# Weight sums of every second feature: made in the output projection instead of the first up stage

## The chip, the cores and the metric

The kernel runs on one core of one Trainium2 chip. The metric is device time in microseconds (us) of one execution. Before the change the median of three runs is 2763.57 us (2761.47 to 2770.18). Engines: PE multiplies matrices (PEld loads its weights), DVE is the vector engine, ACT the scalar engine, POOL the GpSimd engine, SP the engine that here only issues transfers. Each engine works through its own queue in order; ACT, POOL and SP also issue DMA transfers from that queue.

## What is computed

One layer of a hybrid encoder on 2048 prompt rows and 8 x 16 sample rows: band attention and an mLSTM side by side, an output projection, then a convolutional feed-forward block.

```python
mix = jnp.concatenate([att, mlstm_out], axis=-1) @ w_out
x = x + rms_norm(mix, norm_g[1])
ffn, new_buf = conv_ffn(rms_norm(x, norm_g[2]), conv_buf, w_up, w_conv, b_conv, w_down)
x = x + rms_norm(ffn, norm_g[3])

def conv_ffn(h, buf, w_up, w_conv, b_conv, w_down):
    u = h @ w_up
    ext = jnp.concatenate([buf, u], axis=1)
    y = b_conv + sum(ext[:, j:j + S] * w_conv[j] for j in range(3))
    gate, up = jnp.split(y, 2, axis=-1)
    return (jax.nn.gelu(gate, approximate=True) * up) @ w_down, ext[:, S:]
```

w_up is 1024 x 5632, that is 22 features of 128 for each of gate and up; w_down is 2816 x 1024. All data are float32.

## The kernel before, in words

**Products.** Every matrix product is made as three matmuls on a high and a low part (`mm3`, lines 104 to 106): an ACT cast makes the high part, a DVE subtraction the low part (`split`, lines 1308 and 1309). The up product of a feature does not multiply four quarter blocks eight times but seven times, by sums of blocks. For each feature f the four blocks of w_up (quads a11, a12, a22, a21, each 128 x 512, 256 KB) need four sums s1 to s4.

**Stages.** After the projections and while the attention still ends, `project` (w_out) runs over 17 row tiles. Each tile has two halves of 512 columns with 8 x 3 matmuls each; `mt` holds the transposed rows of a tile (PE transposes `mT_pt`, ACT cast at line 210, DVE low part at line 211), `mx` takes a half's sum from PSUM (line 1026), `mr` is the scaled input of a later tile. Beside the tiles of the second half, units of `h2_units` prepare the feed-forward input (`x2r`, `h2T_pt`, `B`). Then come three row blocks, each with an up stage over 22 features and a down stage. Block 0's down stage takes two halves (dh) of 22 k-steps with 18 matmuls each; blocks 1 and 2 use a seven-product form of the down product too, which needs folded blocks of w_down, kept in `wtd`.

**Where sums are made.** In block 0, `load_quads` loads a feature's four quads through SP (line 1320), makes s1 to s4 on DVE (line 1325) and stores them through POOL to `wsd` (line 1327); blocks 1 and 2 load quads and stored sums back (line 1336). The generator `folds` does the like for the 11 blocks of w_down, during block 0's down stage, one step after each k-step: at step 0 two loads on ACT's queue (line 1175), at step 1 the other two, at step 3 four operations on DVE (line 1180) and four stores on POOL (line 1185). Its tiles come from the pool `spare` with six places, used in turn; `quad` has 11 places.

**What sets the order.** The kernel is written as generators that are interleaved by hand; a scheduler then orders each engine's queue. Instructions wrapped in `keep_in_program_order` keep their place in the order in which the program was written.

Of the kernel before, what the change touches and what calls it, by code (L numbers as in the profile page):

```python
# [39 lines left out]
PAIRS = [[(((b[j], 0), (b[j + 3], 0)), j * P, P, f"{b[j]}") for j in range(3)] for b in FBLOCKS[:2]]  # L40
NK = NF // 2
FAST = (1, 2)
ORDERS = [[f for k in range(NK) for f in (k, k + NK)] if b in FAST else list(range(NF)) for b in range(3)]
# [6 lines left out]
def hymba_step(ctx: ExitStack, tc: tile.TileContext, I: dict, O: dict):  # L50
# [923 lines left out]
    def project(tiles):  # L974
# [25 lines left out]
        def turn_rows(s):  # L1000
            rows_to_T(s.m, s.mt, 0, f"mT{s.t}", ps_mm if s.t < 8 else ps_big)

        load(ss[0])
        norm(ss[0])
# [4 lines left out]
        for n_, s in enumerate(ss):  # L1009
# [7 lines left out]
            for hf in range(2):  # L1017
                c = slice(hf * 512, hf * 512 + 512)
                acc = ps_mm(f"wo{t}_{hf}")
                for k in range(KT):  # L1020
                    mm3(acc, s.mt[:, 0, k, :], s.mt[:, 1, k, :], wo[k][0][:, c], wo[k][1][:, c],
                        start=(k == 0), stop=(k == KT - 1))
                    if k % 4 == 3:
                        yield 2.6, 0.5
                ssq = small.tile([P, 1], F32, tag="wssq", name=f"wssq{t}_{hf}")
# [12 lines left out]
            nc.vector.scalar_tensor_tensor(xr, m, rs, xr, op0=ALU.mult, op1=ALU.add)  # L1038
            nc.sync.dma_start(x2d[t], xr)


# [124 lines left out]

    def folds(period, plan):

        live = {}

        def load(k, xs):
            if k < NK:
                for x in xs:
                    live[k, x] = spare_tile(f"fold{k}_{x}")
                    tc.keep_in_program_order(nc.scalar.dma_start(live[k, x], I["w_down"][k][:, x * 512:(x + 1) * 512]))

        def combine(k):
            a, b, c, d = [live[k, x] for x in range(4)]
            for o, x, y in ((a, b, a), (b, c, b), (c, a, c), (d, d, c)):
                tc.keep_in_program_order(nc.vector.tensor_tensor(o, x, y, op=ALU.add if o is d else ALU.subtract))  # L1180

        def store(k):
            if k >= 0:
                for x in range(4):
                    tc.keep_in_program_order(nc.gpsimd.dma_start(wtd[k][:, x * 512:(x + 1) * 512], live.pop((k, x))))
# [127 lines left out]
    def load_quads(b, f, g):  # L1313

        src = lambda i: I["w_up"][f][:, i * 512:(i + 1) * 512]
        if b == 0 and g == 0:
            q = []
# [11 lines left out]
            return [a11, s2, s3, s1]  # L1329
        if b == 0:  # L1330
            return raws.pop(f)
# [125 lines left out]
    unfinished = []  # L1457
    fold = folds(4, {0: ("ab",), 1: ("cd",), 3: ("combine", "store")})

# [6 lines left out]
    for b, tiles in enumerate(FBLOCKS):  # L1466
# [344 lines left out]
        for dh in range(2):  # L1811
# [9 lines left out]
            for c in range(6):  # L1821
# [35 lines left out]
                for k in ks:  # L1857
                    if (dh, k) not in parts:
                        split_g(dh, k, w3_tile)
                    if dh == 1 or k >= 3:  # L1860
                        fetch(dh + (k + 2) // NF, (k + 2) % NF)
                    for j in order if k == NF - 1 else range(nt):
                        down(j, k, wh, wl)
                    if k >= 1:
                        ahead.step()
                    if b == 0:
                        next(fold, None)
            if tail:
                continue
# [117 lines left out]
```

## Time and profile before

| | |
|---|---|
| median of three runs | 2763.57 us |
| the profiled execution's own time | 2763.96 us |
| its span, first to last instruction | 2762.2 us, mean granted clock 0.997 |
| PE busy in the span | 2692.4 us (97%) |
| DVE, ACT, POOL busy | 1902.5 us (69%), 1437.1 us (52%), 627.4 us (23%) |
| DMA traffic | 539.72 MB, mean 195 GB/s |
| w_out, its matmuls | from 1053.9 to 1318.3 us |
| block 0, up stage | from 1319.4 to about 1640 us |
| block 0, down stage | from 1639.2 to about 1839 us |

The profile is one execution. A row of a stretch of time gives, for each engine, its busy time and the count of its instructions in that stretch. A row of waits reads: who waited, for whom, us in total, how often, the longest. A row of a tile gives the shortest, middle and longest duration in ns and the first and last start in us. A row of the timeline gives start, duration, engine, line and operation, and in brackets how long the engine had idled and what ended that. A transfer's time to landing runs from its issue until its data are there.

### The profile page before, as it was taken

To read this page: it belongs to the slowest core of one execution; us is meant where nothing else is said; L and a number is where in the kernel's file an instruction comes from. 1 tells how busy PE (TensorE), PEld (TensorE's weight loads), DVE (VectorE), ACT (ScalarE), POOL (GpSimd) and SP (SyncE) were. 2 spreads that over 40 slices of the span, in tenths; PEclk is the share of its full clock that TensorE was granted. 3 is DMA by queue.
4 is the path that set the end of the run, shared out by engine and by line. 5 is a ranking of instruction groups with operands and counts; after the bars stand their busy time and mean duration, and the time that the engine had idled before them with its cause. 6 is when DMAs were issued, how large, how long until landed. Compare 5 with 4: busy or idle time off the path is not lost.

```text
span 2762.2 us, 47713 instructions
## 1 busy us (share of the span) xinstructions
PE 2692.4 (97%) x16422; PEld 2520.0 (91%) x16422; DVE 1902.5 (69%) x3593; ACT 1437.1 (52%) x2918; POOL 627.4 (23%) x1276
## 2 busy tenths in 40 slices
PE   7899999999999999999999999999999999999998
PEld 7899999998899998888999998789999878999976
DVE  5345445646546567655999988558888875998956
ACT  4355545635356566544554555435554665555554
POOL 1000010211100011222333322123443212555401
PEclk9999999999999999999999999999999999999999
DMA  5534355547564456355645559867886777788775
GB/s 180 161 117 137 106 158 166 170 146 215 155 187 132 139 169 196 120 171 177 239 166 182 166 174 337 297 230 202 242 241 189 244 238 245 217 261 247 249 264 184
DMA packets 329185, 539.72 MB, mean 195 GB/s; under 512 B 60354, under 2 KB 162974, under 8 KB 328814
## 3 DMA queue, kind: packets, MB, share of 16 engines
q1 hardware_dynamic: 248382, 393.82, 46.1%
q0 software_dynamic: 35632, 97.48, 11.3%
q10 hardware_dynamic: 44928, 45.37, 5.0%
q8 instruction: 129, 2.11, 0.3%
q14 instruction: 114, 0.93, 0.1%
HBM read 383.28 MB, written 162.68 MB: 198 GB/s over the span
## 4 chain that ended last, share of the span: by engine, by line
PE 79%; DMA 10%; DVE 5%; ACT 2%; issue 2%; POOL 1%; SPq 0%; ACTq 0%; DVEq 0%; POOLq 0%
PE uec L104 6%; PE uec L105 6%; PE uec L106 6%; PE dn L106 4%; PE dn L104 4%; PE dn L105 4%; PE ua L106 3%; PE ua L105 3%; PE ua L104 3%; PE qb L105 2%; PE qb L106 2%; PE qb L104 2%; PE pt L76 2%; PE wo L106 2%; PE wo L105 2%
## 5 line engine op out<-in xcount | busy, mean ns | idle before, releaser
L104 PE MATMUL uec<-B,wuh 128*128 128x384 f32 (+1 forms) x720 | 236.0, 328 | 2.5 <-DVE uu L1645 2.5
L105 PE MATMUL uec<-B,wuh 128*128 128x384 f32 (+1 forms) x720 | 235.1, 327 | 0.0
L106 PE MATMUL uec<-B,wul 128*128 128x384 f32 (+1 forms) x720 | 233.7, 327 | 0.0
L1308 ACT CAST wuh<-wu 128x512 fp32r<-128x512 f32 x255 | 141.7, 618 | 107.8 <-PE uec L105 98.6
L1309 DVE TENSOR_TENSOR wul<-wu,wuh 128x512 fp32r<-128x512 f32 x255 | 165.1, 683 | 3.7 <-DMA x2d<-mx 2.3
L405 DVE CUSTOM_DVE_ANT_0 tmp<-s,nb 128x640 f32<-128x640 f32 (+4 forms) x128 | 94.4, 737 | 93.9 <-PE s L395 92.1
L104 PE MATMUL vo<-wi_h,hT 128*128 128x256 f32 x544 | 155.2, 285 | 0.7 <-DVE mt L211 0.6
L106 PE MATMUL vo<-wi_h,hT 128*128 128x256 f32 x544 | 155.6, 286 | 0.0
L105 PE MATMUL vo<-wi_l,hT 128*128 128x256 f32 x544 | 154.8, 285 | 0.0
L104 PEld LDWEIGHTS uec<-B,wuh 128*128 128x128 f32 x720 | 135.1, 188 | 5.4 <-DVE uu L1645 4.1
L104 PE MATMUL qk<-hT,wi_h 128*128 128x384 f32 (+1 forms) x384 | 128.5, 335 | 7.4 <-ACT qk_st L236 6.7
L105 PEld LDWEIGHTS uec<-B,wuh 128*128 128x128 f32 x720 | 135.2, 188 | 0.2
L106 PEld LDWEIGHTS uec<-B,wul 128*128 128x128 f32 x720 | 135.1, 188 | 0.0
L418 DVE TENSOR_TENSOR ptl<-pt,pth 128x640 fp32r<-128x640 f32 (+4 forms) x128 | 93.6, 738 | 57.4 <-ACT pth L417 56.4
L406 ACT ACTIVATE tmp<-tmp,mn 128x640 f32<-128x640 f32 (+4 forms) x128 | 97.6, 763 | 66.1 <-DVE mn L405 64.7
L1309 DVE TENSOR_TENSOR wdl<-wdr,wdh 128x512 fp32r<-128x512 f32 x198 | 125.0, 685 | 7.8 <-ACT wdh L1308 7.6
L105 PE MATMUL qb<-hT,wi_h 128*128 128x384 f32 (+1 forms) x384 | 127.9, 333 | 0.0
L105 PE MATMUL qk<-hT,wi_h 128*128 128x384 f32 (+1 forms) x384 | 127.8, 333 | 0.0
L106 PE MATMUL qk<-hT,wi_l 128*128 128x384 f32 (+1 forms) x384 | 127.4, 332 | 0.0
L106 PE MATMUL qb<-hT,wi_l 128*128 128x384 f32 (+1 forms) x384 | 127.3, 331 | 0.0
L104 PE MATMUL qb<-hT,wi_h 128*128 128x384 f32 (+1 forms) x384 | 127.2, 331 | 0.0
L106 PE MATMUL dn<-wdh,al 128*128 128x512 f32 x308 | 124.1, 403 | 2.6 <-DVE al L1309 2.6
(447 smaller groups left out, 9271.1 us busy)
## 6 DMA issues: line engine op xcount, KB each, us to landing
wu<-in_w_up SPq DMA_DIRECT2D x220, 256.0 KB, 4.9
wu<-wsd SPq DMA_DIRECT2D x176, 256.0 KB, 5.0
wdr<-in_w_down SPq DMA_DIRECT2D x110, 256.0 KB, 5.3
wi_raw<-in_w_in SPq DMA_DIRECT2D x52, 512.0 KB, 4.0
wsd<-ws POOLq DMA_DIRECT2D x88, 256.0 KB, 3.8
wdr<-wtd SPq DMA_DIRECT2D x88, 256.0 KB, 5.3
gr<-gd SPq DMA_DIRECT2D x39, 384.0 KB, 6.1
kraw<-kTd SPq DMA_DIRECT2D x112, 128.0 KB, 3.3
```

Source lines behind the costliest of these rows:

```text
L76: nc.tensor.transpose(out, in_, ident[:n, :n])
L104: nc.tensor.matmul(out, ah, bh, start=start, stop=False, skip_group_check=onto)
L105: nc.tensor.matmul(out, ah, bl, start=False, stop=False, skip_group_check=onto)
L106: nc.tensor.matmul(out, al, bh, start=False, stop=stop, skip_group_check=onto)
L405: nc.vector.tensor_tensor_reduce(o_, s_, b_, 1.0, 3e38, ALU.add, ALU.min, accum_out=mn)
L406: nc.scalar.activation(tmp[:, :n], tmp[:, :n], AF.Exp, bias=mn, scale=-1.0, accum_out=rsum[:, i % 4, hh:hh + 1])
L418: nc.vector.tensor_tensor(s.ptl[:, sl, qc], ptv, s.pth[:, sl, qc], op=ALU.subtract)
L1308: nc.scalar.copy(h, r)
L1309: nc.vector.tensor_tensor(l, r, h, op=ALU.subtract)
```

## The change

`folds` becomes a generator over a list of units and now makes both kinds of sums: "T" for a block of w_down, "U" for a feature of w_up. It advances by six steps for a unit: two loads, nothing, two loads, and then one DVE operation a step; the fourth operation and the four stores come at the first step of the next unit. `project` advances a "U" fold for the odd features (`UPS`) by one step after each four k's of a half, which makes four steps to a tile and 68 in all, against 66 for the 11 units. In block 0, `load_quads` then treats an odd feature as blocks 1 and 2 do: it loads quads and stored sums, seven loads in place of four, and makes no sums. In block 0's down stage the "T" fold is advanced once after each even k-step and twice after each odd one, so that a unit still takes four k-steps.

```diff
+UPS = [1, 3, 5, 7, 9, 11, 13, 15, 17, 19, 21]
+WOUT_FOLDS = [("U", f) for f in UPS]
...
+        fold, owed = folds(WOUT_FOLDS), [0.0]
         load(ss[0])
...
                     if k % 4 == 3:
+                        owed[0] += 6 * len(WOUT_FOLDS) / 66
+                        while owed[0] >= 1:
+                            owed[0] -= 1
+                            next(fold, None)
                         yield 2.6, 0.5
...
+        for _ in fold:
+            pass
...
-    def folds(period, plan):
...
-        acts = dict(ab=lambda k: load(k, (0, 1)), cd=lambda k: load(k, (2, 3)), combine=combine, store=store,
-                    before=lambda k: store(k - 1))
-        for k in range(NK):
-            for step in range(period):
-                for what in plan.get(step, ()):
-                    acts[what](k)
+    def folds(units):
+
+        keep = tc.keep_in_program_order
+        sub, plus = ALU.subtract, ALU.add
+        ahead = None
+        for n_, (what, k) in enumerate(units):
+            src, dst = (I["w_down"], wtd) if what == "T" else (I["w_up"], wsd)
+            part = lambda d, x: d[k][:, x * 512:(x + 1) * 512]
+            if ahead:
+                ahead()
+            q = [spare_tile(f"fold{what}{k}_{x}") for x in range(2)]
+            for x in range(2):
+                keep(nc.scalar.dma_start(q[x], part(src, x)))
+            yield
+            yield
+            q += [spare_tile(f"fold{what}{k}_{x}") for x in (2, 3)]
+            for x in (2, 3):
+                keep(nc.scalar.dma_start(q[x], part(src, x)))
+            yield
+            a, b, c, d = q
+            if what == "T":
+                ops = [(a, b, a, sub), (b, c, b, sub), (c, a, c, sub), (d, d, c, plus)]
+                out = [a, b, c, d]
+            else:
+                ops = [(c, d, c, plus), (d, a, d, sub), (a, c, a, sub), (b, b, a, sub)]
+                out = [a, d, c, b]
+            for o, x, y, op in ops[:3]:
+                keep(nc.vector.tensor_tensor(o, x, y, op=op))
                 yield
-        if live:
-            store(NK - 1)
+
+            def ahead(out=out, dst=dst, k=k, last=ops[3]):
+                o, x, y, op = last
+                keep(nc.vector.tensor_tensor(o, x, y, op=op))
+                for i, t in enumerate(out):
+                    keep(nc.gpsimd.dma_start(dst[k][:, i * 512:(i + 1) * 512], t))
+        ahead()
...
-        if b == 0 and g == 0:
+        if b == 0 and g == 0 and f not in UPS:
...
-        if b == 0:
+        if b == 0 and f not in UPS:
             return raws.pop(f)
...
-    fold = folds(4, {0: ("ab",), 1: ("cd",), 3: ("combine", "store")})
+    fold = folds([("T", k) for k in range(NK)])
...
                     if b == 0:
                         next(fold, None)
+                        if k % 2:
+                            next(fold, None)
```

The line numbers of the changed kernel are higher: by 2 in the first thousand lines, by 7 in the tail of `project`, by 9 in `h2_units`, by 16 from `load_quads` on. What stands on three engines at one place of w_out, near the change of stages to the feed-forward block, is shown next.

DVE in w_out, around the sample tile (16) while `mt8`, the next tile's rows, is made; `mx16` takes tile 16's two halves from PSUM, `x2r` are rows of `h2_units`. Before:

```order
L997 TENSOR_SCALAR mr8_15162<-mr8_15162,att8_rs_15203 128x512
L1026 TENSOR_TENSOR mx16_15206<-wo16_0_15208,norm_row1_13117 128x512
L1098 SCALAR_TENSOR_TENSOR x2r0_15263<-x2r0_15263,n2_0_rs_15286,g2_15160 128x1024
L1098 SCALAR_TENSOR_TENSOR x2r3_15265<-x2r3_15265,n2_3_rs_15292,g2_15160 128x1024
L211 TENSOR_TENSOR mt8_15198<-mT8_pt0_15237,mt8_15198 128x1024
L1026 TENSOR_TENSOR mx16_15206<-wo16_1_15250,norm_row1_13117 128x512
```

And with the change:

```order
L999 TENSOR_SCALAR mr8_15237<-mr8_15237,att8_rs_15287 128x512
L1203 TENSOR_TENSOR foldU11_2_15305<-foldU11_3_15306,foldU11_2_15305 128x512
L1033 TENSOR_TENSOR mx16_15290<-wo16_0_15292,norm_row1_13117 128x512
L1107 SCALAR_TENSOR_TENSOR x2r0_15353<-x2r0_15353,n2_0_rs_15377,g2_15235 128x1024
L1107 SCALAR_TENSOR_TENSOR x2r3_15355<-x2r3_15355,n2_3_rs_15383,g2_15235 128x1024
L213 TENSOR_TENSOR mt8_15282<-mT8_pt0_15326,mt8_15282 128x1024
L1203 TENSOR_TENSOR foldU11_3_15306<-foldU11_0_15257,foldU11_3_15306 128x512
L1033 TENSOR_TENSOR mx16_15290<-wo16_1_15339,norm_row1_13117 128x512
```

The first sum of feature 11, which needs the third and the fourth quad, stands ahead of tile 16's first evacuation and of `mt8`; the second sum stands ahead of the second evacuation.

ACT one tile later, in tile 8; `wssq` are the squares of a half, `b2` and `B` belong to `h2_units`. Before:

```order
L1123 COPY b220_15394<-h2T_pt0_1_1_15389 128x512
L1028 ACTIVATE mx8_15311,wssq8_0_15349<-wo8_0_15313 128x512
L1118 CAST B1_0_15280<-t20_15396 128x4x128
L1118 CAST B2_0_15281<-t30_15397 128x4x128
L210 CAST mt9_15303<-mT9_pt0_15353 128x1024
```

And with the change:

```order
L1035 ACTIVATE mt16_15149,wssq16_1_15385<-wo16_1_15339 128x512
L997 ACTIVATE mt9_15394,assq9_15395<-mr9_15337 128x512
L1188 DMA foldU13_0_15422<-in_w_up 128x512
L1188 DMA foldU13_1_15423<-in_w_up 128x512
L1127 CAST B1_0_15371<-t20_15500 128x4x128
L1127 CAST B2_0_15372<-t30_15501 128x4x128
L1193 DMA foldU13_2_15489<-in_w_up 128x512
L1193 DMA foldU13_3_15490<-in_w_up 128x512
L1035 ACTIVATE mx8_15402,wssq8_0_15449<-wo8_0_15404 128x512
L212 CAST mt9_15394<-mT9_pt0_15453 128x1024
```

The four loads of feature 13 stand in ACT's queue ahead of the squares of tile 8's first half and of the cast of `mt9`.

PE at the same place, in the second half of tile 8 (`wo8_1`), with the transposes for tile 9 (`mT9_pt0`). Before:

```order
L105 MATMUL wo8_1_15376<-wo3_13516,mt8_15198 128x512
L106 MATMUL wo8_1_15376<-wo3_13516,mt8_15198 128x512
L76 MATMUL mT9_pt0_15353<-ident_72,mr9_15248 128x128 x8
L104 MATMUL wo8_1_15376<-wo3_13516,mt8_15198 128x512
L105 MATMUL wo8_1_15376<-wo3_13516,mt8_15198 128x512
```

And with the change:

```order
L106 MATMUL wo8_1_15476<-wo6_13592,mt8_15282 128x512
L107 MATMUL wo8_1_15476<-wo6_13592,mt8_15282 128x512
L78 MATMUL mT9_pt0_15453<-ident_72,mr9_15337 128x128 x8
L108 MATMUL wo8_1_15476<-wo6_13592,mt8_15282 128x512
L1115 MATMUL h2T_pt0_0_1_15522<-ident_72,x2r0_15353 128x128 x4
L106 MATMUL wo9_0_15552<-wo0_13379,mt9_15394 128x512
L107 MATMUL wo9_0_15552<-wo0_13379,mt9_15394 128x512
```

Before, twelve matmuls of `wo8_1` and a group of four transposes stand between `mT9_pt0` and the first use of `mt9`; with the change one matmul and that group.

More of the change, by code (lines that the diff above doesn't have):

```diff
@@ L1165, in late_B @@
             nc.vector.tensor_tensor(lo, lo.bitcast(F32), hi, op=ALU.subtract)
-    def folds(period, plan):
[L1169 to L1185, printed above, removed]
-        acts = dict(ab=lambda k: load(k, (0, 1)), cd=lambda k: load(k, (2, 3)), combine=combine, store=store,
-                    before=lambda k: store(k - 1))
-        for k in range(NK):
-            for step in range(period):
-                for what in plan.get(step, ()):
-                    acts[what](k)
-                yield
-        if live:
-            store(NK - 1)
```

## The prediction

> **What bounds the kernel now.** I read the stages first: busy time by engine in the three stretches that the change touches (w_out with the tail of the attention, the up stage of block 0, the down stage of block 0). Columns: span, then PE, PEld, DVE, ACT, POOL busy with counts, clock, DMA share, GB/s.
>
> ```profile
> 1053.00:1312.00 259.00, 255.51 (x1389) 215.40 (x1389) 159.32 (x296) 129.90 (x313) 62.60 (x119) 1.00 0.50 161
> 1312.00:1645.00 333.00, 331.96 (x1878) 326.85 (x1877) 306.17 (x465) 169.90 (x273) 111.99 (x193) 1.00 0.54 183
> 1645.00:1865.00 220.00, 214.61 (x992) 179.16 (x991) 149.35 (x217) 104.50 (x182) 48.94 (x95) 1.00 0.84 285
> ```
>
> PE sets the end in all three, at full granted clock. It idles 259.00 - 255.51 = 3.5 us in w_out, 1.0 us in up 0 and 5.4 us in down 0: together 9.9 us, and no rearrangement of DVE, ACT or DMA work can win more than that here. DVE, at 306 of 333 us, is nearly full in up 0, yet PE hardly waits for it; its room is in w_out (99.7 us idle). Then I read what PE waited for, w_out first, then down 0 (us in total, times, longest).
>
> ```profile
> PE wo L106 <- DVE mt L211: 1.2, 3, 0.5
> PEld wo L106 <- DVE mt L211: 2.4, 3, 0.9
> ...
> PE dn L104 <- DVE fr L1393: 2.0, 2, 1.5
> PE h2T_pt L1106 <- ACT b L1123: 1.7, 1, 1.7
> PE h2T_pt L1106 <- DVE t L1132: 0.8, 1, 0.8
> ```
>
> In w_out the wait that recurs is for mt, the transposed rows of the next tile. So I followed one late tile (start, duration, engine, line): transposes, ACT cast, DVE low part, and the evacuation that shows when the second half of the current tile has ended on PE.
>
> ```profile
> 1252.23 1.04 PE L76 MATMUL mT_pt<-ident,mr 128*128 128x128 f32 x8
> ...
> 1253.36 1.02 ACT L210 CAST mt<-mT_pt 128x1024 fp32r<-128x1024 f32 x1 [2.59 <-PE mT_pt L76]
> ...
> 1254.41 1.23 DVE L211 TENSOR_TENSOR mt<-mT_pt,mt 128x1024 fp32r<-128x1024 f32 x1 [4.41 <-ACT mt L210]
> ...
> 1256.75 0.68 DVE L1026 TENSOR_TENSOR mx<-wo,norm_row 128x512 f32<-128x512 f32 x1
> ```
>
> The low part is done at 1255.64, and wo's second half at about 1256.75: a margin of 1.1 us before PE stands. That is thin, although DVE had idled 4.41 us just before. The rows of six such tiles give the pace and the cover:
>
> ```profile
> L210 ACT CAST mt<-mT_pt x6: 1006/1014/1016, 1227.6 to 1292.7; 128x1024 fp32r<-128x1024 f32 x6
> ...
>   ACT mt L210: 19.1, 6
> ```
>
> (1292.7 - 1227.6) / 5 = 13.0 us a tile; DVE idles 19.1 / 6 = 3.2 us a tile just before mt. With four fold steps to a tile, a step is 3.25 us.
>
> **The change, part by part.** First, what leaves up 0. The sums of one feature are four DVE operations and four POOL issues:
>
> ```profile
> L1325 DVE TENSOR_TENSOR ws<-wu,wu x44: 678/683/693, 1304.4 to 1611.3; 128x512 f32<-128x512 f32 x44
> 1312.00:1645.00 333.00, 56.66 (x84) 1.00 0.54 183
> L1327 POOL DMA_DIRECT2D wsd<-ws x84 | 45.7, 544 | 86.0 <-DVE ws L1325 82.4 <-DVE ug L1483 2.1 <-DVE x L1622 0.7
> ```
>
> Half of the 22 features go, 44 operations x 0.683 = 30.1 us of DVE (84 of the 88 lie inside the stretch, the rest just before it) and 44 x 0.544 = 23.9 us of POOL. SP gets three loads more for each odd feature, 33 in all; SP issues them ahead, and the stage's DMA share of 0.54 has room, since 44 stores leave it. What the path can gain is PE's idle time in the stage, at least 0 and at most 1.0 us. I take -1.0. Where cover is concerned: an odd feature's stored sums must have landed before SP's in-order queue reaches them; they were stored tens of us earlier, except feature 21's, which is used last.
>
> Second, what enters w_out: 44 ACT loads, 44 DVE operations, 44 POOL stores. In volume it fits: 159.3 + 30.1 = 189 of 259 us of DVE. The price is in order, since these are in-order queues with waits. A unit takes six steps: first two loads (and the last sum and four stores of the unit before) at step 0, the other two loads at step 2, three sums at steps 3, 4, 5. The pool of spare tiles has six places, so the loads at step 2 reuse the places of quads whose stores were issued at step 0, and ACT stands until those have landed; the sum at step 3 needs exactly these loads, and DVE stands until they have. The nearest rows for the parts of this chain:
>
> ```profile
> L1175 ACTq DMA_DIRECT2D fold<-in_w_down x44: 334/335/852, 1649.8 to 1825.2; - x44
> L1180 DVE TENSOR_TENSOR fold<-fold,fold x44: 674/684/694, 1656.8 to 1838.5; 128x512 f32<-128x512 f32 x44
> L1185 POOL DMA_DIRECT2D wtd<-fold x44: 542/542/608, 1661.3 to 1839.5; - x44
> ...
> DMA to landing us min/median/max: 3.1/6.4/9.7
> ```
>
> Those are the folds of the down stage; the weight sums' own stores and the weight loads (median us from issue to landing; the first store row is of up 0, the second of w_out's end):
>
> ```profile
> wsd<-ws POOLq DMA_DIRECT2D x84, 256.0 KB, 3.7
> wsd<-ws POOLq DMA_DIRECT2D x4, 256.0 KB, 6.5
> wu<-in_w_up SPq DMA_DIRECT2D x220, 256.0 KB, 4.9
> ```
>
> Last sum 0.68, four store issues 4 x 0.54 = 2.17 (the fourth store is that of the quad whose place is wanted last), landing 3.7 to 6.5, load issue 0.33, landing 4.9: 11.8 to 14.6 us after step 0, while step 3 comes 3 x 3.25 = 9.8 us after it. So DVE stands 2.0 to 4.8 us at the first sum of a late unit, and behind it in its queue are mx (the evacuation of wo) and mt, for which PE waits. The cover is DVE's own idle time ahead of mt, 3.2 us, plus the margin of 1.1: 4.3 us. The excess is 0 at the one end and 0.5 us at the other; without that cover (the hold falls on top of the tile's other work) it is 4.8 - 1.1 = 3.7 us. Bounds over 11 units: 0 to 41 us. A gain is excluded, as nothing leaves this stage. I take 0.6 us a unit, next to the covered end because the idle before mt is in every one of the six rows, and a little above it because a sum of 0.68 itself also falls between two steps of the chain: 11 x 0.6 = 6.6 us. The place on PE where the transposes now stand one wo matmul and four short transposes ahead of their use is inside this: cast 1.02 and low part 1.23 against a margin that has gone.
>
> A rule of the Trainium skill speaks on this chain. DMA: Bandwidth & Descriptors, section "Anatomy of one DMA", fits a transfer as 2.0 us plus its bytes over 436 GB/s; my estimate from that page is 2.6 us for 256 KB, and the chain would be 0.68 + 2.17 + 2.6 + 0.33 + 2.6 = 8.4 us, inside the 9.8, so that nothing would wait. The trace differs: its medians are 3.7 to 6.5. The sum by that rule would be -1.0 instead of +5.6.
>
> Third, down 0. Bursts of four sums become single sums; loads, stores and volume stay. But the distance from the stores of a unit to the loads that reuse their places shrinks from two k-steps to one. A k-step is the distance of two gh casts, and ACT already waits here for such stores (us, times, longest):
>
> ```profile
> 1732.99 0.83 ACT L1308 CAST gh<-gr 128x768 fp32r<-128x768 f32 x1 [3.33 <-PE dn L105]
> 1737.14 0.84 ACT L1308 CAST gh<-gr 128x768 fp32r<-128x768 f32 x1 [1.24 <-PE dn L105]
> ACT gh L1308 <- DMA wtd<-fold: 13.6, 3, 4.9
> ```
>
> So each of 11 units has 4.15 us less. Behind the standing loads are gh and wdh, the next weights' casts. The lower bound is -5.4 (all PE idle gone, the single sums leave room at the boundary of the two halves, where 1.5 + 1.7 + 0.8 of it lies). For the upper, today's 13.6 us of such waits stand beside at most 5.4 us of PE idle, a ratio of 0.4; 11 x 4.15 x 0.4 = 18 us. I take 0: the instructions of ACT and DVE stand almost as before, casts run two k-steps ahead, and the boundary wait comes from SP's loads, which do not move.
>
> Sum: -1.0 + 6.6 + 0 = +5.6 us on the profiled execution's 2763.96 us (span 2762.2), so 2769.6; that execution lies 0.4 above the median of the runs, 2763.57, which gives **2769 us**.
>
> **The rivals.**
>
> 1. All covered. Stores and loads land as fast as the shortest of the weight sums' transfers in this trace,
>
> ```profile
> DMA to landing us min/median/max: 2.3/3.8/9.7
> ```
>
> so the chain is 0.68 + 2.17 + 2.3 + 0.33 + 2.3 = 7.8 us, under 9.8, nothing waits in w_out, and up 0 gives its 1.0: 2763. For it: DVE's 99.7 us of idle time in w_out. Against it: the medians. Chance 0.18. The Trainium skill's fit, named above, leads here too.
> 2. The boundary in down 0 goes as well, 4.0 us, and most of the rest of PE's 9.9: 2754 to 2757. Against it: SP's order there. Beyond -0.3% it needs 8.3 of 9.9 us. Chance 0.08.
> 3. Slower: DVE is held at the first sum, with mt behind it. The place is DVE in w_out's late tiles; it decides from a store landing of about 6 us on, as with w_out's own four stores (6.5), when the cover of 4.3 us is used up. Priced midway between the covered excess and the uncovered one, (0.5 + 3.7) / 2 = 2.1 us a unit, it is 11 x 2.1 = 23 us, less 1.0 of up 0: 2786. For it: the margin of only 1.1 us. Against it: DVE's idle time before mt. Chance 0.28.
> 4. Slower in down 0: ACT stands at the reused places, and PE's dn follows. Half of the bound, 9 us, on top of the forecast's 5.6: 2778. For it: the 13.6 us of today. Against it: the loads' place in ACT's order, which stays. Chance 0.12.
>
> That the change does not do what it says is no rival: the diff removes the sums of the odd features from up 0 and makes the same four in w_out.
>
> **How the numbers follow.** The forecast, a loss between 0 and 8 us, has the remaining 0.34; its own range is 2763 to 2772. A measurement of this kernel can tell about 0.3%, or 8.3 us, from no change. Faster by more than that is rival 2, 0.08; within it lie the forecast and rival 1, 0.34 + 0.18 = 0.52; slower are rivals 3 and 4, 0.28 + 0.12 = 0.40. The range for 8 in 10 runs from 2757, where rival 2 ends, to 2790, a little above rival 3.
>
> **What would show it.** In up 0: DVE busy about 276 of some 333 us, PE idle under 1 us, sums down to x44. In w_out: 44 sums of 0.68, DVE busy near 189, waits of DVE for the fold's loads and of ACT for the stores, PE waits for mt up from 1.2 to some 6 us; if there are none, rival 1 holds, and if they pass 20 us, rival 3. In down 0: the wait of gh for wtd's stores near 13.6; doubled, with dn behind, it is rival 4. The prediction is wrong if up 0 shortens by more than 2 us (PE then had hidden cost there) or if the span changes outside 1053 to 1865.

## The result: slower, and the profile after

The changed kernel takes 2800.44 us (median of 6 runs, 2796.05 to 2805.34), the kernel before 2767.06 us beside it (6 runs). The ratio is 1.0125, with a 95% interval of 1.0113 to 1.0137: 33 us slower. The profiled execution of the changed kernel took 2805.32 us, its span is 2803.6 us.

The stages come first, each from its own first matmul to that of the next: w_out, up stage of block 0, down stage of block 0. The rows of the down stage end 2.2 us ahead of that, in both kernels alike. The columns are span, then PE, PEld, DVE, ACT and POOL busy with counts, clock, DMA share, GB/s. Before:

```profile
1053.90:1319.40 265.50, 262.01 (x1416) 220.50 (x1415) 162.06 (x301) 129.87 (x314) 62.80 (x120) 1.00 0.51 165
1319.40:1639.20 319.80, 319.10 (x1823) 316.75 (x1822) 297.00 (x450) 166.73 (x267) 110.83 (x190) 1.00 0.54 181
1639.20:1836.90 197.70, 191.97 (x857) 155.77 (x856) 136.72 (x196) 93.09 (x157) 38.26 (x73) 1.00 0.86 289
```

The same stages of the changed kernel:

```profile
1052.30:1352.50 300.20, 273.75 (x1415) 227.58 (x1414) 184.54 (x342) 129.06 (x314) 84.83 (x165) 0.96 0.67 219
1352.50:1671.40 318.90, 317.93 (x1824) 317.29 (x1823) 278.37 (x414) 168.02 (x267) 73.57 (x146) 1.00 0.54 176
1671.40:1876.10 204.70, 195.57 (x857) 158.70 (x856) 135.37 (x194) 93.18 (x157) 35.68 (x70) 0.97 0.83 279
```

w_out is 34.7 us longer, up 0 is 0.9 shorter, down 0 is 7.0 longer; what lies ahead of w_out is 1.6 shorter and what lies behind down 0 is 2.2 longer. Together that is 41.4 us, the difference of the two spans (2803.6 - 2762.2); the profiled execution stands 4.9 us above its median, that of the kernel before 3.1 below its own.

The 34.7 us of w_out have two halves that are read differently. PE's idle time went from 265.50 - 262.01 = 3.5 to 300.20 - 273.75 = 26.5 us, 23.0 more. And PE's busy time grew by 11.7 us with the same matmuls (1416 counted before, 1415 after): the granted clock of the stage is 0.96 where it was 1.00. What PE waited for in w_out (us in total, times, longest):

```profile
PE wo L108 <- DVE mt L213: 7.8, 2, 4.1
PE h2T_pt L1115 <- DVE x2r L1107: 7.4, 1, 7.4
PE ot L432 <- ACT pth L419: 3.9, 1, 3.9
```

So it is not a little at each unit: four stops (3.9, 7.4, 4.1 and 3.8) make 19 of the 26.5 us. They lie at three places.

**Tile 1, near 1085 us.** ACT's timeline before:

```profile
1080.68 0.37 ACT L715 ACTIVATE num<-ma,colsp 128x129 f32<-128x129 f32 x1 [3.74 <-DVE cst L713]
1081.52 1.29 ACT L417 CAST pth<-pt 128x640 fp32r<-128x640 f32 x2 [0.47 <-PE ot L430]
...
1083.70 0.41 ACT L660 ACTIVATE mvo<-mvo 128x256 f32<-128x256 f32 x1
```

and in the changed kernel:

```profile
1082.62 0.37 ACT L717 ACTIVATE num<-ma,colsp 128x129 f32<-128x129 f32 x1 [2.01 <-DVE cst L715]
1083.22 0.60 ACT L1035 ACTIVATE mx<-wo 128x512 f32<-128x512 f32 x1 [0.23 <-DVE mx L1033]
...
1086.28 0.42 ACT L662 ACTIVATE mvo<-mvo 128x256 f32<-128x256 f32 x1 [2.38 <-DMA mvo<-vobd]
...
1087.19 0.67 ACT L419 CAST pth<-pt 128x640 fp32r<-128x640 f32 x1
```

pth (the attention weights of the last heads, for which PE's `ot` waits) stood directly behind num. Now mx and mvo stand between, mvo waits 2.38 us for its load (vobd, which is no load of the folds), and pth comes 4.6 us behind num instead of 0.8. The scheduler has put ACT's instructions into another order around the fold's loads.

**Tile 8, 1218 to 1234 us.** DVE's timeline at the first sum of a unit; its last two loads were issued on ACT's queue from 1217.89 on:

```profile
1227.99 0.69 DVE L1203 TENSOR_TENSOR foldU<-foldU,foldU 128x512 f32<-128x512 f32 x1 [8.56 <-DMA foldU<-in_w_up]
1228.60 0.68 DVE L1033 TENSOR_TENSOR mx<-wo,norm_row 128x512 f32<-128x512 f32 x1
1232.04 1.28 DVE L1107 SCALAR_TENSOR_TENSOR x2r<-x2r,n_rs,g 128x1024 f32<-128x1024 f32 x1 [2.75 <-POOL n_rs L95]
```

DVE stands 8.56 us: ACT had waited 1.3 us before it issued the two loads (1216.6 to 1217.9), and some 9 us passed until the sum had them. Behind it is mx, behind mx is ACT's mx (12.78 us idle), then the square sums of x2r, POOL's n_rs, DVE's x2r, and PE at last. Over w_out DVE stood at sums for loads in six of the eleven units:

```profile
DVE foldU L1203 <- DMA foldU<-in_w_up: 19.4, 6, 8.6
```

What PE did after that stop (start, duration):

```profile
1233.47 1.09 PE L1115 MATMUL h2T_pt<-ident,x2r 128*128 128x128 f32 x4 [7.39 <-DVE x2r L1107]
1234.21 0.78 PE L106 MATMUL wo<-wo,mt 128*128 128x512 f32 x1
1234.78 0.63 PE L107 MATMUL wo<-wo,mt 128*128 128x512 f32 x1
...
1238.58 0.39 PE L106 MATMUL wo<-wo,mt 128*128 128x512 f32 x1
```

The same matmul takes 0.78, 0.63 and, five us later, 0.39 us: the clock is lower after the stop and comes back. The next unit's first sum held DVE 4.11 us at 1254, with mt right behind it: PE's stop of 4.1. Here the loads were issued late: ACT stood 5.77 us around them, by the trace until the stores from the places that they reuse had landed. ACT and DVE (the cast for mt ends at 1250.30):

```profile
1244.68 2.33 ACTq L1193 DMA_DIRECT2D foldU<-in_w_up  x2
1247.11 0.60 ACT L1035 ACTIVATE mx<-wo 128x512 f32<-128x512 f32 x1 [5.77 <-DMA wsd<-foldU]
1249.28 1.02 ACT L212 CAST mt<-mT_pt 128x1024 fp32r<-128x1024 f32 x1 [1.48 <-PE mT_pt L78]
1254.33 0.69 DVE L1203 TENSOR_TENSOR foldU<-foldU,foldU 128x512 f32<-128x512 f32 x1 [4.11 <-DMA foldU<-in_w_up]
1254.94 1.22 DVE L213 TENSOR_TENSOR mt<-mT_pt,mt 128x1024 fp32r<-128x1024 f32 x1
```

**The last tile, near 1336 us.** Here the held operation is not a fold but the up stage's own first sum, whose load landed late; it held DVE 2.90 us in the kernel before:

```profile
1336.02 0.69 DVE L1341 TENSOR_TENSOR ws<-wu,wu 128x512 f32<-128x512 f32 x1 [5.63 <-DMA wu<-in_w_up]
...
1338.55 1.22 DVE L213 TENSOR_TENSOR mt<-mT_pt,mt 128x1024 fp32r<-128x1024 f32 x1
```

The clock in slices of 10 us around two of the stops:

```profile
1220.00:1230.00 10.00, 6.08 (x31) 4.68 (x29) 1.29 (x2) 0.63 (x3) 0.00 (x0) 1.00 0.90 319
1230.00:1240.00 10.00, 6.47 (x25) 5.25 (x26) 7.25 (x10) 6.83 (x14) 3.67 (x7) 0.66 0.11 32
...
1250.00:1260.00 10.00, 5.26 (x13) 3.65 (x14) 5.89 (x8) 4.39 (x10) 3.04 (x8) 0.76 0.92 328
```

The DMA share of 0.90 with 319 GB/s in the first slice is the burst in which the loads of the first hold landed: x2r, g and x2d of the other work are in flight with them.

### The profile page after: what moved, and what is told of

It reads as the page before. It is cut to its first block, busy times and chain, and to the rows that moved or that the text cites. A ratio compares the mean times of both kernels' runs of the same rounds, so it can differ in the third digit from the quotient of the medians.

```text
span 2803.6 us, 47833 instructions
## 1 busy us (share of the span) xinstructions
PE 2706.6 (97%) x16422; PEld 2529.4 (90%) x16422; DVE 1904.9 (68%) x3593; ACT 1437.2 (51%) x2918; POOL 613.3 (22%) x1276
## 4 chain that ended last, share of the span: by engine, by line
PE 45%; DMA 5%; DVE 2%; issue 1%; ACT 1%; POOL 1%; SPq 0%; DVEq 0%; POOLq 0%; ACTq 0%
PE uec L106 5%; PE uec L107 5%; PE uec L108 5%; PE dn L108 3%; PE dn L106 3%; PE dn L107 3%; PE ua L108 3%; PE ua L107 3%; PE ua L106 3%; PE dnm L108 1%; PE ub L106 1%; PE ub L108 1%; PE ub L107 1%; PE dnm L107 1%; PE dnm L106 1%
## 5 line engine op out<-in xcount | busy, mean ns | idle before, releaser
L1324 ACT CAST wuh<-wu 128x512 fp32r<-128x512 f32 x284 | 156.7, 617 | 107.6 <-PE uec L107 98.2
L1325 DVE TENSOR_TENSOR wul<-wu,wuh 128x512 fp32r<-128x512 f32 x284 | 183.3, 686 | 2.3 <-ACT wuh L1324 1.2
L1325 DVE TENSOR_TENSOR al<-ar,ah 128x768 fp32r<-128x768 f32 (+2 forms) x94 | 71.0, 765 | 81.4 <-ACT ah L1324 81.1
```

The lines of the kernel that those rows point to most:

```text
L1324: nc.scalar.copy(h, r)
L1325: nc.vector.tensor_tensor(l, r, h, op=ALU.subtract)
```

## The experiments

The theory at first was: a sum reads loads that were issued one step earlier, DVE stands there, and the units cost 2 to 3 us each. Its rivals were the DVE volume, the traffic, the reused places and the down stage. In the diffs, "old folds" stands for the generator and the plan of the kernel before, kept for block 0's down stage.

| run | change against before | ratio, 95% interval | us | w_out of the profiled execution |
|---|---|---|---|---|
| changed kernel | all | 1.0125 (1.0113 to 1.0137) | +33.4 | 300.2 |
| u_only | new sums in w_out | 1.0110 (1.0092 to 1.0128) | +30.8 | 296.5 |
| t_only | new folds in down 0 | 1.0002 (0.9990 to 1.0013) | +0.2 | 264.5 |
| dve_only | 44 sums, no transfers | 1.0012 (1.0003 to 1.0022) | +3.4 | 268.6 |
| stores_only | 44 stores on POOL | 1.0025 (1.0011 to 1.0039) | +6.9 | 267.6 |
| loads_only | 44 loads on ACT | 1.0065 (1.0047 to 1.0083) | +18.2 | 278.7 |
| moves_only | loads and stores | 1.0075 (1.0058 to 1.0091) | +20.0 | 280.4 |
| loads_pool | 44 loads on POOL | 0.9998 (0.9988 to 1.0008) | -1.7 | 266.3 |
| loads_sp | 44 loads on SP | 1.0027 (1.0018 to 1.0036) | +8.1 | 270.6 |
| loads_tiny | 44 loads of 8 KB on ACT | 1.0003 (0.9994 to 1.0012) | +1.2 | 266.7 |
| loads_first | u_only, load three steps ahead | 1.0104 (1.0083 to 1.0125) | +30.3 | 282.3 |
| u_skip8 | u_only, three steps left out | 1.0117 (1.0095 to 1.0138) | +29.9 | 280.0 |
| u_skip8_again | the same kernel | 1.0099 (1.0079 to 1.0119) | +27.8 | 282.0 |
| early4 | four units, tiles 1 to 7 | 1.0029 (1.0017 to 1.0040) | +8.5 | 267.0 |
| u_late_start | u_only, started six steps later | 1.0029 (1.0018 to 1.0040) | +8.2 | 272.7 |
| u_pool | u_only, loads on POOL | 1.0034 (1.0017 to 1.0052) | +12.9 | 272.4 |
| u_sp | u_only, loads on SP | 1.0068 (1.0053 to 1.0083) | +19.9 | 281.0 |
| u_loads_free | u_only, loads placed by the scheduler | 1.0092 (1.0077 to 1.0107) | +25.6 | 283.8 |
| u_free | u_only, all placed by the scheduler | 1.0091 (1.0069 to 1.0114) | +25.5 | 265.2 |

"us" is the difference of the medians of the run and of the kernel before, run beside it; the ratio is worked out otherwise, and for u_pool it gives 9.4 us instead of 12.9. The last column is of one execution each and stands at 265.5 in the kernel before. It need not follow the medians. What lies ahead of w_out, where only u_loads_free and u_free place units, took 1046.5 to 1055.5 us in the other profiled executions, so a few us of a total need not be the effect of a version.

### Which part: u_only and t_only

```diff
 u_only, in block 0:
-    fold = folds([("T", k) for k in range(NK)])
+    fold = folds_old(4, {0: ("ab",), 1: ("cd",), 3: ("combine", "store")})
 t_only:
-UPS = [1, 3, 5, 7, 9, 11, 13, 15, 17, 19, 21]
+UPS = []
```

> The sums of the 11 odd features are made in w_out as in the change, but block 0's down stage keeps its old plan of folds (two k-steps from store to reload, four sums in one burst). If the loss belongs to w_out (PE's idle time there grew from 3.5 to 26.5 us and its busy time by 12 us at a lower granted clock), this run keeps nearly all of it: 26 to 36 us above the kernel before, PE idle in w_out over 15 us, and PE idle in down 0 back near 5.7 us. If the down stage carried it, at most 15 us above.

> No odd feature is moved (w_out and up 0 as before); only block 0's down stage makes its folds one operation at a time, with one k-step from store to reload. If the loss belongs to w_out: 0 to 6 us above the kernel before, with PE idle in down 0 near 9 us and DVE waiting there for the fold's loads (9.1 us in the changed kernel). If the shorter distance is a main cost: 12 us or more above.

Both as expected of the loss in w_out: 30.8 us in the one, 0.2 in the other. PE's idle time in w_out is 25.2 us in u_only, in three of the four stops of the changed kernel (7.4, 4.1, 4.3) and a smaller fourth (2.1). The folds one operation at a time cost nothing alone; PE's idle time in t_only's down 0 is 5.3 us, not the 9 expected. In the changed kernel down 0 took 7.0 us more, with one stop of 3.7 us; the two ratios differ by 0.0015, 4 us, inside their intervals, so whether that is in every execution is open.

### Volume: dve_only, stores_only, loads_only, moves_only

```diff
 the kernel before, in project, after each four k's:
+                        next(extra, None)
 dve_only, at steps 3, 4, 5 and 6 of a unit:
+                keep(nc.vector.tensor_tensor(t, t, t, op=ALU.subtract))
 loads_only and moves_only, two at steps 0 and 2:
+                keep(nc.scalar.dma_start(t, I["w_up"][f][:, x * 512:(x + 1) * 512]))
 stores_only and moves_only, four at the next unit's step 0:
+                keep(nc.gpsimd.dma_start(wsx[f - 2][:, x * 512:(x + 1) * 512], t))
```

> The kernel before, with 44 more DVE sums of one 128x512 tile in w_out at the steps where the change makes its sums; they read a tile that was filled once, so no load, no store and no wait for a transfer comes with them. Late loads as the cause: the 30 us of DVE work alone fit into DVE's 100 us of idle time, -2 to +6 us. DVE volume, or one more operation ahead of mt, as the cause: 15 us or more above.

> The kernel before with 44 stores on POOL's queue in w_out, four at every sixth step, from tiles filled once, to a scratch tensor; no loads, no sums. If the stores carry the cost of the moves (POOL's statistics stand behind 4 x 0.54 us of issues, and the traffic of the bursts of four): 10 us or more above the kernel before. If the loads carry it: -2 to +5 us. If only both together fill the queues, this run and the one with loads alone stay each under 6 us.

> The kernel before with the change's 44 loads on ACT's queue in w_out at the same steps, no sums and no stores. The moves with loads and stores cost 20.0 us. If the loads in ACT's queue (its order around them, and their traffic) carry that: 10 us or more above the kernel before, with PE standing for pth near 1085 us again (3.5 us). If the stores on POOL's queue carry it: -2 to +5 us.

> The kernel before, with the change's 44 loads on ACT's queue and 44 stores on POOL's queue in w_out at the same steps, to a scratch tensor, and no sums. If DVE standing at a sum whose load is late is the cause, PE loses little here: 0 to 12 us above the kernel before. If the traffic itself (transfers of x, of vobd and of the first weights that land later) or ACT standing at reused places is the cause: 20 us or more above.

DVE volume is excluded as the cause (+3.4). The theory misses in moves_only: 20.0 us without a single sum. The loads carry 18.2 of them, as the one side of their expectation had it; the stores' 6.9 lie between their two bounds, and the parts do not add up (18.2 and 6.9 alone, 20.0 together). In loads_only PE's stops in w_out were:

```profile
PE ot L430 <- ACT pth L417: 3.5, 1, 3.5
PE wo L106 <- DVE mt L211: 3.1, 2, 2.8
```

the first and the last place, without tile 8's. That left the bytes and the queue.

### Bytes or queue: loads_pool, loads_tiny, loads_sp

```diff
-                keep(nc.scalar.dma_start(t, ...))
+                keep(nc.gpsimd.dma_start(t, ...))      loads_pool
+                keep(nc.sync.dma_start(t, ...))        loads_sp
+                keep(nc.scalar.dma_start(t[:, 0:16], ...))   loads_tiny
```

> The kernel with loads alone, its 44 loads issued on POOL's queue instead of ACT's; same steps, same bytes, no sums, no stores. With loads on ACT's queue the scheduler placed pth, for which PE's next product waits, behind mx and mvo in ACT's order near 1085 us; in this kernel ACT's order there is that of the kernel before. If ACT's order around the loads carries the 18.2 us: +3 to +9 us (what 44 issues on POOL cost in the run of stores alone, 6.9), with no stop for pth. If the bytes of the loads, which make other transfers land later, carry it: +14 us or more.

> The kernel with loads alone on ACT's queue, each load cut to 16 of 512 columns (8 KB instead of 256 KB). If the bytes carry the 18.2 us: -2 to +5 us. If the issues in ACT's queue and the order that the scheduler makes around them carry it: +10 us or more, with stops at other places than 1220 and 1320 us.

> The kernel before with 44 loads of 256 KB on SP's queue in w_out, no sums, no stores. No instruction is added to ACT's queue, but the scheduler's order of ACT near 1085 us has mx and mvo ahead of pth, as with loads on ACT's queue; with loads on POOL's queue it had not, and cost 0. If that order by itself stops PE: PE stands for pth there (2 us or more), and the total is 6 us or more above the kernel before. If only loads in ACT's own queue do it: no stop for pth and under 4 us.

The bytes by themselves are excluded: loads_pool moves the same 44 x 256 KB at the same steps, the stage's DMA share is up from 0.51 to 0.66, and nothing is lost.

```profile
1054.30:1320.60 266.30, 262.47 (x1414) 220.09 (x1413) 161.28 (x301) 130.03 (x314) 87.69 (x165) 1.00 0.66 208
```

loads_sp shows the first place alone. It adds nothing to ACT's queue, but the scheduler puts mx (here ahead of num as well) and mvo ahead of pth there too, and PE stands:

```profile
1080.69 0.58 PE L430 MATMUL ot<-pth,vhl 128*128 128x256 f32 x1 [3.92 <-ACT pth L417]
```

It costs 8.1 us, and no other stop of w_out in it is longer than 0.8 us. Its w_out is 5.1 us longer than before; where the other 3 us lie is not shown. Nor does mvo ahead of pth stop PE every time. In loads_tiny, whose order is another again (mvo ahead of pth, mx behind), ACT stood longer for it, and PE's wait for pth was 0.6 us:

```profile
1082.43 0.42 ACT L660 ACTIVATE mvo<-mvo 128x256 f32<-128x256 f32 x1 [4.43 <-DMA mvo<-vobd]
```

loads_tiny costs nothing: the issues by themselves are free. By its own expectation that speaks for the bytes; together with loads_pool it says that neither the issues nor the bytes cost anything alone, and that full loads in ACT's or SP's queue do, with the orders made around them. Order and bytes changed together there, so it decides no more. loads_only's further 10 us over loads_sp are loads in ACT's own queue and the orders made around them; ACT stood once for 5.0 us at such a load. Which of the two it is stays open.

### The distance from load to sum: loads_first and u_skip8

```diff
 loads_first:
-            q = [spare_tile(f"fold{what}{k}_{x}") for x in range(2)]
-            for x in range(2):
+            q = [spare_tile(f"fold{what}{k}_{x}") for x in range(4)]
+            for x in range(4):
                 keep(nc.scalar.dma_start(q[x], part(src, x)))
 u_skip8:
-                        owed[0] += 6 * len(WOUT_FOLDS) / 66
+                        owed[0] += 0 if (n_, hf, k) in ((8, 0, 7), (8, 1, 3), (8, 1, 7)) else 1
```

> Sums of the 11 odd features in w_out, the down stage's folds by the old plan. A unit issues its four loads at step 0, makes two sums at step 3 and two at step 4 with the four stores; so each sum reads a load of at least three steps before (about 10 us in the late tiles) instead of one, while the distance from a store to the load that reuses its place stays two steps. If DVE standing at a sum whose load came one step earlier makes the third of the loss that the moves alone don't show (30.8 - 20.0 us), this run comes to 16 to 24 us above the kernel before and DVE's wait at the sums for loads falls from 19.4 us to under 5. If the reused places hold it: 28 us or more above, with ACT standing at the loads.

> The sums of the 11 odd features in w_out, down stage by the old plan (30.8 us above the kernel before), except that three steps are left out in tile 8 (after the second group of k's of its first half and both of its second half), so that the unit whose first sum stood 8.8 us for its loads beside the transfers of x2r has three more steps between those loads and that sum; later units follow three steps later. Same sums, loads, stores and queues; ACT's order near 1085 us unchanged. If that one hold on DVE, and the lower clock after it, are the second cause: the stop for x2r falls from 7.4 us to under 2.5 and the total to 16 to 23 us above the kernel before, with the stop for pth (4.3 us) still there. If the loss comes with the units wherever they stand: 27 us or more above.

> The same kernel as the last one, for a second profiled execution: the first took 2785.2 us, the others of that run 2793.3 to 2802.4, so one profile may not show what the median holds. If other executions hold DVE again (the landing of the loads differs from execution to execution), a profile above 2790 us shows PE stops in w_out of more than 16 us in all, and which they are; if it comes out near 2785 again, the stop for x2r stays under 2.5 us and the difference to the median stays open. Total of the runs: 2785 to 2802 us as before.

Their profiled executions show what was expected, their medians don't. In loads_first DVE's wait at the sums fell from 21.0 us in u_only to 2.4:

```profile
DVE foldU L1197 <- DMA foldU<-in_w_up: 2.4, 2, 2.1
```

and w_out from 296.5 to 282.3; in u_skip8 the stop for x2r is 0.8 us (0.7 in its second profile), the stop for mt at 1254 us is 0.5, and w_out is 280.0 and 282.0, with the stop for pth still there (3.3 and 3.5). So DVE's hold is what stops PE in tile 8. Without it w_out is 14 to 17 us shorter in these profiles, though not all of that is the hold's: the stop for pth is shorter too, 1.9 us in loads_first. But the median of loads_first is 30.3 us above the kernel before, and that of u_skip8 29.9 and 27.8, against 30.8 of u_only. For u_skip8 a part is seen: the steps that were put off fall behind the last tile, and the first 30 us of up 0, here in the second profile, have a PE idle time of 5.5 us at a clock of 0.89, so that up 0 takes 326.9 us (326.4 in the first profile) instead of u_only's 318.9, and half of what w_out wins is lost again. For loads_first no profile shows where its other executions (2793 to 2796 us against the profiled 2786.3) lose; the record has only their mean granted clock, 0.991 to 0.992 against 0.995. That stays open, and so the medians do not bear out that the hold in tile 8 carries a large part of the loss.

### Other places and queues: early4, u_late_start, u_pool, u_sp, u_loads_free, u_free

```diff
 early4 (UPS = [1, 5, 9, 13]):
+                        owed[0] += 1 if (1, 1) <= (n_, hf) <= (7, 1) else 0
 u_late_start:
+                        owed[0] += 66 / 61 if n_ >= 1 and (n_, hf) >= (1, 1) else 0
 u_pool, u_sp (two places each):
-                keep(nc.scalar.dma_start(q[x], part(src, x)))
+                keep(nc.gpsimd.dma_start(q[x], part(src, x)))      u_sp: nc.sync
 u_loads_free (u_free: sums and stores as well):
+                nc.scalar.dma_start(q[x], part(src, x))
```

> Only four features (1, 5, 9, 13) are made in w_out, at the change's own pace of one step after each four k's, but only from the second half of tile 1 to the end of tile 7 (about 1100 to 1214 us in the changed kernel's trace); the other seven odd features are made in block 0 as before; the down stage's folds by the old plan. The changed kernel lost PE time at three places in w_out (1084 to 1088, 1226 to 1256, 1335 to 1340 us) and little between. If the loss is one of places where other transfers are due at once: -3 to +4 us. If each unit costs alike, 30.8 / 11 = 2.8 us: +8 us or more.

> The sums of the 11 odd features in w_out with loads on ACT's queue, down stage by the old plan, but the first step is made in the second half of tile 1 instead of the first half of tile 0, and the 66 steps follow a little closer. ACT's order near 1085 us is then that of the kernel before. If that order is one of three separate causes: the stop for pth is gone and the total is 6 to 12 us less than the 30.8, so 19 to 25 us above the kernel before, with the stops at x2r and mt of the late tiles still there. If it is the loads in ACT's queue anywhere: 28 us or more above.

> The sums of the 11 odd features in w_out, the down stage's folds by the old plan (30.8 us above the kernel before), with the 44 loads on POOL's queue instead of ACT's. The order of ACT near 1085 us is that of the kernel before. If the queue of the loads carries most of the loss: 3 to 15 us above the kernel before (44 sums alone cost 3.3, 44 stores alone 6.9), with no stop for pth. If DVE standing at the sums carries it whatever the queue: 20 us or more above.

> As the last one, with the 44 loads on SP's queue, where they stand behind SP's waits for x2d's stores. The scheduler still places pth behind mx and mvo in ACT's queue near 1085 us. Expected: the stop for pth there again (3 us or more), loads landing later than on ACT's queue, and 25 us or more above the kernel before. If only ACT's standing at its own loads mattered: under 15 us.

> The sums of the 11 odd features in w_out with the down stage's folds by the old plan (30.8 us above the kernel before), but the loads on ACT's queue are not held at their place in the program: the scheduler may place them earlier, as soon as the place in the pool is free. The first six then stand at the program's start and the rest of them somewhat ahead of the sums that read them. If late loads and the order around them carry the loss: under +20 us, with DVE's wait at the sums for loads under 8 us. If the traffic does: +26 us or more.

> As the last one, with loads, sums and stores all free to be placed by the scheduler: it puts the units at the start of the program (the first 190 or so of DVE's instructions) instead of w_out, where they meet other transfers. If the loss of the change belongs to w_out's late tiles: w_out near 265 us again, and the total -3 to +8 us, with what is lost now lost in the first 150 us. If the sums cost the same wherever they stand: +20 us or more.

u_late_start says most. All eleven units, the same loads on ACT's queue, the same sums and stores, only begun six steps later and a little closer together (66/61): 22.6 of the 30.8 us are gone, more than the 6 to 12 expected. ACT's order at tile 1 is that of the kernel before and the stop for pth is 0.3 us; and the units now meet the tiles at other steps. DVE still waits 12.8 us at sums, in w_out as a whole, but never long:

```profile
DVE foldU L1203 <- DMA foldU<-in_w_up: 12.8, 6, 3.6
```

The longest wait is 3.6 us instead of 8.8, and PE's longest stop for mt is 2.0. u_only has 21.0 us of such waits and 25.2 us of PE's idle time in w_out, u_late_start 12.8 and 7.2. It takes away the stop for pth and the long hold at once, so it does not tell their shares; no run changes ACT's order at tile 1 alone.

early4 loses no more in w_out than 1.5 us (267.0), yet 8.5 in all, just inside the side of its expectation on which each unit costs alike; its profiled execution, the slowest of its runs, has up 0 at 325.0 us, and that was not followed further. u_pool has no stop for pth and costs 12.9 us, u_sp has it again (3.6) and costs 19.9: the queue of the loads matters, less than was expected of u_sp. u_loads_free missed its bound: ACT then stood at loads for reused places (5.6, 4.8 and 2.2 us). u_free has w_out at 265.2 us as before, but 25.5 us in all, as the side expected on which the sums cost the same wherever they stand: its units lie in the program's first 200 us, where PE is busy 165.2 us instead of 178.2.

No version was faster than the kernel before, and none can gain more than up 0's 0.7 us of idle time by moving its sums.

## Why the prediction was wrong

What bounds the kernel was read rightly: PE everywhere, and no more than 9.9 us to win. **Up 0** was right: -1.0 forecast, -0.9 measured, though DVE lost 18.6 us of work there and POOL 37.3. **Down 0** alone was right too: 0 forecast, 0.2 us in t_only.

**w_out is where it failed**: +6.6 forecast, +34.7 measured. The step is "I take 0.6 us a unit, next to the covered end". A part of the loss came by the named mechanism, and rival 3 had its place, DVE held at the first sum with mt (and mx) behind it. Three things were wrong in the sum.

1. *A mean instead of a worst case, and a cover that was not there.* The chain was priced with a landing of 4.9 us, the median of the weight loads, and an excess per unit over a cover of 4.3 us. The eleven units did wait 19.4 us in all, 1.8 on average, less than the 2.0 to 4.8 of the forecast for a late one. But one of them waited 8.56 us, with its loads in a burst with x2r, and PE stopped for 7.39 us. The next one waited 4.11 us, inside the cover, and PE stopped for 4.05: the cast for mt had ended when DVE's hold began, so no idle time of DVE was left ahead of mt to take it up. Behind the four shorter holds, up to 3.17 us, PE shows no stop. The row with the spread (3.1/6.4/9.7) stood in the prediction; its upper end belonged into the sum for the unit that meets x2r. The landings that the trace gives for the transfers of the changed kernel's folds, loads and stores, spread the same way:

```profile
DMA to landing us min/median/max: 2.6/4.7/11.0
```

The 2.6 us that the prediction estimates from the Trainium skill (DMA: Bandwidth & Descriptors, section "Anatomy of one DMA") is the time of the fastest of them. The stores' landing, which rival 3 took as its condition, had its part in the second hold (ACT's 5.77 us at the reused places) and little in the first (1.3 us). loads_first keeps the distance from store to load and lost DVE's waits, but it also gives the loads more time ahead of the sums, so it does not separate the two.

2. *An order that was not compared.* The forecast looked at the order around tile 16 and at DVE, ACT and PE there, and took the rest of w_out as unmoved. In tile 1 the scheduler had put pth behind mx and mvo in ACT's queue: 3.9 us of PE's idle time, and no rival held it. Where it is the only long stop of w_out (loads_sp), w_out is 5.1 us and the whole 8.1 us longer; what the order costs by itself no run shows. It is seen without a time, in the order of the two kernels on ACT in the tail of the attention.
3. *The price of a stop.* A stop was priced at its own length. After a long stop PE runs at a lower clock for some us; over w_out that is 11.7 us beside 23.0 of idle time, half as much again. The trace of the kernel before shows it already, in its last stage (PE, start and duration):

```profile
2634.00 0.50 PE L104 MATMUL dn<-wdh,ah 128*128 128x512 f32 x1 [2.06 <-ACT ah L1308]
2634.34 0.40 PE L105 MATMUL dn<-wdl,ah 128*128 128x512 f32 x1
2635.00 0.80 PE L106 MATMUL dn<-wdh,al 128*128 128x512 f32 x1 [0.26 <-DVE al L1309]
2635.59 0.63 PE L104 MATMUL dn<-wdh,ah 128*128 128x512 f32 x1
```

A stop of 2.06 us, and the next matmuls take 0.63 instead of 0.39. The Trainium skill has the rule: TensorE: Matmul & The Clock Gate, Part 1 (section "The HAM clock gate (the "warmup" mystery)"), says that the array falls to half its clock after an idle window of about 3.4 us and comes back after about 3.4 us of sustained work. Behind a stop of 2.04 us in u_late_start (shown in the last section) matmuls start 0.42 us apart and 3.4 us later 0.23, which agrees nearly with the half and with the time to come back; the stops of 2.04 and 2.06 are shorter than the page's window and lowered the clock all the same. So here a stop of 2 us can bring the lower clock. It does not every time: after one of 3.02 us, earlier in the trace of the kernel before, the clock is 1.00 in the next 8 us.

```profile
110.54 0.44 PE L104 MATMUL qk<-hT,wi_h 128*128 128x384 f32 x1 [3.02 <-ACT qk_st L236]
110.54:118.54 8.00, 8.00 (x55) 8.00 (x56) 2.39 (x6) 3.61 (x10) 1.12 (x3) 1.00 0.36 109
```

So rival 3's price, 23 us in eleven equal parts, came nearest partly by luck: the two long holds at fold sums stopped PE for 11.4 of the 23.0 us by which its idle time grew, ACT's order and the late load of the up stage made most of the rest, and the lower clock added its 11.7. By the prediction's own sign the forecast would have seemed right: PE's waits for DVE's mt grew to 7.8 us, near the 6 of the forecast and far from the 20 of rival 3. The loss came where no sign looked, at x2r, at pth and in the clock. How the medians divide among these causes stays open. Rival 1 (all covered) failed on two units; rival 2 had nothing in it, as up 0 gave its 1 us and no more. Rival 4 is not confirmed: t_only excludes it as a cost of the shorter distance alone, the wait of gh for the stores of wtd, its sign, fell from 13.6 to 5.0 us, and the 3.7 us of the changed kernel's down 0 are one execution's.

## What to carry to other kernels

Where work is put into in-order queues beside a bound engine, look for the longest single hold, not only for the sum of all: in the traces here cover swallowed the short ones, and the two long ones went through and were paid again in part by the lower clock. Compare the order of every engine over the whole stage in which code is inserted, since the scheduler moves others as well. Moving the start of the sequence by six steps won back more here (22.6 of 30.8 us) than any change of the sequence itself, and it is a cheap experiment. A profile is one execution: loads_first and u_skip8 were 8 and 10 us faster in theirs than in the median of their runs.

## What was not expected of the hardware

44 loads of 256 KB, 11.5 MB in 266 us, are free on POOL's queue (ratio 0.9998, DMA share 0.51 to 0.66) and cost 18.2 us on ACT's, at the same steps. And the clock after a stop: it doesn't follow the stop's length alone. It stayed at 1.00 after the stop of 3.02 us above, and in u_late_start it is low for 3.4 us after one of 2.04 us,

```profile
1309.63 0.54 PE L108 MATMUL wo<-wo,mt 128*128 128x512 f32 x1 [2.04 <-DVE mt L213]
1309.97 0.63 PE L106 MATMUL wo<-wo,mt 128*128 128x512 f32 x1
1310.39 0.63 PE L107 MATMUL wo<-wo,mt 128*128 128x512 f32 x1
...
1313.38 0.40 PE L108 MATMUL wo<-wo,mt 128*128 128x512 f32 x1
1313.61 0.40 PE L106 MATMUL wo<-wo,mt 128*128 128x512 f32 x1
```

so that stop costs 2.0 us and some 1.7 more (0.83 over the 10 us behind it), almost its own length again.
